# Down projection of an encoder block: where the sums of weight quarters are made

## The chip, the cores and the metric

The kernel runs on one core of a Trainium2 chip. The metric is the device time of one execution in microseconds (us). The kernel before takes 1648.68 us, the median of three runs (1645.87, 1648.68 and 1654.98 us).

## The reference, cut to what matters

Two layers of an encoder on 512 tokens of width 1024, all in float32. A layer is a token mixer (neighbourhood attention in layer 0, dilated attention in layer 1) and a SwiGLU channel mixer with 2816 hidden columns:

```
def swiglu(x, w_gate, w_up, w_down):
    return (jax.nn.silu(x @ w_gate) * (x @ w_up)) @ w_down

x = x + rms_norm(h, norm_mix_post[layer])
h = rms_norm(x, norm_ffn_pre[layer])
x = x + rms_norm(swiglu(h, w_gate, w_up, w_down), norm_ffn_post[layer])
```

The change concerns the last product, hidden (512 x 2816) by `w_down` (2816 x 1024), and what is issued during the two products ahead of it.

## The kernel before, in words

**Exactness.** Every float32 operand is split into a high part and a low remainder (`split`: ScalarE copies and rounds, line 89; VectorE subtracts, line 90). One product is three matmuls: high by high, high by low, low by high (`mm3`, lines 101 to 103).

**Seven products instead of eight.** Each large product is cut into 2 x 2 quarters and done in seven block products from sums of quarters. In the down projection the hidden matrix lies as four quarters `x1a, x1b, x2a, x2b` (two halves of tokens by two halves of the contraction), and `w_down` as four quarters `ga, gb, ua, ub` (two halves of columns by two halves of the contraction). A weight quarter is 128 partitions by 2 x 2816 float32, 2.88 MB. The seven products, in the order of the code, take the weights gb, ga, ga+ua, ga+ua+ub, ub, ua+ub and the sum of all four. Their names in the profile carry p2, p1, d, s2/s4, s3 and x2b.

**Pieces.** `down` (line 582) takes each product in six pieces, five of two 128-row blocks and one of one block. A whole piece is 512 KB of weights and 12 matmuls with 512 columns; a product is 66 matmuls. Products p1, s2, s3 and x2b accumulate in the banks called `left` (tile `yd_s`), p2, d1 and s4 in `right` (`yd_pp`).

**Where the weight sums come from.** Plain quarters are loaded by SyncE (SP) into buffers of 4 KB per partition: four halves of the `raw` tiles (tiles `r_d`), later two more from the arena `raw` (`more`). The sums are made in SBUF: `ga` is loaded whole into the arena `wd` (`mem`, line 648), and GpSimd (POOL) issues accumulating DMAs that add `ua`, then `ub`, then `gb` to it piece by piece (line 600). Each needs the split of the earlier sum to be done. For s3, `ua` is loaded into the ring and `ub` added to it there (lines 606 to 608).

**Gate and up.** `gate_up` (line 538) runs 22 units, each from 1 MB of weights (`load2`, line 85). The raw weights go to two `raw` tiles (`r_gu`) and three places in the arena `fg`. POOL makes two of each unit's weight sums (lines 168 and 169). `fg` is one tile, so what is placed over it after it, the arenas `wd` and `raw`, waits for the last unit's last operation (line 564).

**What sets the order.** Python emits the instructions in program order with the position as priority. A planner (line 1186, `schedule_with_timeline_sim=True`) then puts each engine's instructions in an order by a simulated timeline: of the instructions whose operands and buffers are ready, the earliest in the program goes first. On the chip each engine and each DMA-issuing queue runs that order and stops at any wait. DMAs that POOL issues go through one software queue (queue 0), SP's through a hardware queue (queue 1); both are worked off by the same 16 DMA engines. The kernel's first loads (`x_cols`, `g_mix_pre`, `na_v`; lines 804 to 809) feed the first norm and the value projection (`v_quarter`); the loops over the attention heads use POOL for sums and scalings (lines 168 to 174, 853) and its DMAs for storing and reloading results (`rvd`, lines 757 and 761).

Of the kernel before, what the change touches and what calls it, by code (L numbers as in the profile page):

```python
# [26 lines left out]
QF = FT * P  # L27
# [11 lines left out]
def encoder_kernel(ctx: ExitStack, tc: tile.TileContext, a: dict, out: bass.AP):  # L39
    nc = tc.nc  # L40
# [497 lines left out]
    def gate_up(layer, xs, hid, fg):  # L538
        wg, wu = a["wg"], a["wu"]
        raws = ring(fg, 0, 2 * D, 3)  # L540
        g_, u_, p5_ = ring(fg, 6 * D, 512, 4), ring(fg, 8 * D, 512, 2), ring(fg, 9 * D, 256, 2)
        v_ = w22_ring(rxc[:, 4 * D:5 * D])
        units, us = {}, {}

        def unit_of(f):
            if f in units or f >= FT:
                return units.get(f)
            raw = load2((wg[layer, f], wu[layer, f]), f"gu{layer}_{f}", None if f % 5 < 2 else next(raws))
            b, g = bank(("s", "s", "pp", "o", "pp", "pp")[f % 6], f"gu{layer}_{f}"), next(g_)

            def sink(n, left, other):
                u = us.get(f)
                if n == 0:
                    act.activation(g[:, :256], other, AF.Copy)
                    dve.tensor_add(g[:, :256], g[:, :256], left)
                elif n == 1:
                    act.activation(u[:, :256], other, AF.Copy)
                    dve.tensor_sub(u[:, :256], u[:, :256], left)  # L558
                elif n == 2:
                    dve.tensor_sub(u[:, 256:], other, left)  # L560
                else:
                    act.activation(g[:, :256], g[:, :256], AF.Silu)
                    act.activation(g[:, 256:], left, AF.Silu)
                    dve.tensor_mul(hid[f], *(v.rearrange("p (h c) -> p h c", h=2) for v in (g, u)))

            units[f] = Seven(raw, b, xs, f"{layer}_{f}", sink, None, next(v_), (pool, pool, dve, dve))
            return units[f]

        ahead = 3
        for f in range(ahead):  # L570
            unit_of(f).first()
        for f in range(FT):
            for i in range(f, min(f + 2, FT)):
                if i not in us:
                    us[i], units[i].p5 = next(u_), next(p5_)
            run(unit_of(f), unit_of(f + 1), unit_of(f + ahead))

    def down(layer, hm, hl_, mem, yp, more, sink):
# [7 lines left out]
        ga, gb, ua, ub = (a["wd"][layer, i] for i in range(4))  # L590

        def xp(v, i):
# [5 lines left out]
        def add(v, src):  # L598

            nc.gpsimd.dma_start(v, src, accum_op=ALU.add)  # L600
# [10 lines left out]
        def added(w):  # L611

            for i in range(last + 1):
                add(wp(mem, i), wp(w, i))
                yield wp(mem, i)

        def operands2(x, w, name):
            h, u = next(hl_), wslot(name)
            nx, nw = x.shape[1], w.shape[1]
            return (split(h[:, :nx], h[:, 512:512 + nx], x), split(u[0][:, :nw], u[1][:, :nw], w))  # L620

        def prod(o, ops, start=False, ms=(0, 1)):
            hs_, us = ops
            n = hs_[0].shape[1] // 256
            for m in ms:
                for k in range(n):
                    mm3(o[m], both(hs_, ALL, slice(k * 256 + m * P, k * 256 + m * P + P)),
                        both(us, ALL, slice(k * 512, k * 512 + 512)), start and k == 0, k == n - 1)
# [13 lines left out]
            prod(right, operands2(xp(x1b, i), w, f"{nm}p2_{i}"), i == 0)  # L642
        for m in range(2):
            act.activation(y1g[m], right[m], AF.Copy)

        early = list(loaded(ga[:, :2 * D]))
        for i in (*range(2, last + 1), 0, 1):
            nc.sync.dma_start(wp(mem, i), wp(ga, i))
# [7 lines left out]
        for i in range(last + 1):  # L656
            t = wp(mem, i)
            add(t, wp(ua, i))
            prod(right, operands2(xp(x2a, i), t, f"{nm}d1_{i}"), i == 0)
            dve.tensor_sub(xp(x2a, i), xp(x2a, i), xp(x1a, i))  # L660
        for m in range(2):
            act.activation(p5[m], right[m], AF.Copy)
        ops = None
        for i, w in enumerate(loaded(ub)):
            w0 = wp(ub, i)
            t = wp(mem, i)
            add(t, w0)
            dve.tensor_add(xp(x1b, i), xp(x2a, i), xp(x1b, i))

            dve.scalar_tensor_tensor(xp(x1a, i), xp(x2a, i), -1.0, xp(x2b, i), op0=ALU.mult, op1=ALU.subtract)  # L670
            prod(left, operands2(xp(x2a, i), t, f"{nm}s2_{i}"))
            if ops:
                prod(right, ops)
            ops = operands2(xp(x1b, i), w, f"{nm}s4_{i}")
        for m in range(2):
            act.activation(y1u[m], left[m], AF.Copy)
        prod(right, ops)
# [89 lines left out]
    def ffn(layer, stack):  # L767
        hl_ = ring(rxc, 0, D, 5)
        rxb = None
        with arena(f"hid{layer}", FT * 512, "right") as hm:  # L770
            h2 = hm.rearrange("p (h x) -> p h x", h=2)
            hid = [h2[:, :, f * 256:f * 256 + 256] for f in range(FT)]
            with arena(f"fg{layer}", 9 * D + 512) as fg:
                gate_up(layer, xs, hid, fg)
            with arena(f"ed{layer}", D, "right") as ed, arena(f"yp{layer}", 2 * D, "right") as yp:
                rcomb = ring(ed, 0, 512, 2)

                def sink(t, xt, hs, gn):
# [412 lines left out]
```

## Time and profile before

| | |
|---|---|
| time, median of three | 1648.68 us |
| the profiled execution: its time, its span | 1645.9 us, 1644.1 us |
| mean granted TensorE clock | 0.978 |
| PE busy | 1536.3 us (93% of the span) |
| VectorE, ScalarE, POOL busy | 77%, 52%, 42% |
| moved by DMA | 208.80 MB, 127 GB/s on average |
| gate and up, then down, layer 0 | about 293 to 542, 542 to 657 us of the span |
| gate and up, then down, layer 1 | about 1273 to 1523, 1523 to 1636 us of the span |

The time is what the run took; the span is from the first to the last instruction of the same execution, so 1.8 us lie around it. Rows by stage give busy time per engine with the number of instructions, then the granted clock (PEclk, 1.00 is full), the mean busy share of the 16 DMA engines and what they moved. A chain of waits follows the work that ended last back from the end. A timeline row gives start, duration, engine, source line and operand names; what stands in brackets is the idle time before it and what ended it.

### The profile page before, as it was taken

Reading aid. Unit: us, or ns where it says so; the run is one execution under the profiler, and the core shown is the slowest. Engines: PE = TensorE matmul, PEld = TensorE weight load, DVE = VectorE, ACT = ScalarE, POOL = GpSimd, SP = SyncE. Lnnn points to the kernel's source line nnn. Section 1 sums busy time; section 2 is a strip of 40 time slices with the busy share of each in tenths; the row PEclk is TensorE's granted clock in tenths of the full one; section 3 lists DMA queues with packets and bytes.
Section 4 is the critical chain, followed back from the end, with each engine's and each line's share of the span. In section 5 each row is a group of like instructions: output and inputs, shape, how many; then the busy total and the mean of one; then the engine's idle time right before and its main releaser. Section 6 shows DMA issues by size and latency. Waiting matters only on the chain.

```text
span 1644.1 us, 28158 instructions
## 1 busy us (share of the span) xinstructions
PE 1536.3 (93%) x10788; PEld 1387.7 (84%) x10788; DVE 1263.6 (77%) x2140; ACT 850.2 (52%) x1659; POOL 685.7 (42%) x622
## 2 busy tenths in 40 slices
PE   7999999799999898879999999999998799999896
PEld 7977767799999686879988887888876799999684
DVE  5478864889998877677688788697865699998866
ACT  5356653455555555434465456455553455555554
POOL 3345432733330122465556655565613633330221
PEclk9999999899999999999999999999999899999999
DMA  4322353322322996545321231221545233323994
GB/s 167 118 66 97 122 202 128 141 78 106 120 83 71 251 239 177 175 133 163 116 84 53 78 116 65 104 77 65 195 140 169 88 103 104 103 78 97 251 243 115
DMA packets 66248, 208.80 MB, mean 127 GB/s; under 512 B 7040, under 2 KB 17280, under 8 KB 66112
## 3 DMA queue, kind: packets, MB, share of 16 engines
q1 hardware_dynamic: 53936, 164.91, 29.4%
q0 software_dynamic: 12032, 41.82, 10.6%
q8 instruction: 85, 1.39, 0.4%
q14 instruction: 51, 0.42, 0.1%
q10 hardware_dynamic: 144, 0.26, 0.0%
HBM read 184.94 MB, written 22.02 MB: 126 GB/s over the span
## 4 chain that ended last, share of the span: by engine, by line
PE 65%; DVE 14%; DMA 9%; issue 6%; POOL 3%; ACT 3%; SPq 0%; POOLq 0%; DVEq 0%; ACTq 0%
PE gu L101 9%; PE gu L102 9%; PE gu L103 9%; PE pp_d L101 3%; PE pp_d L103 3%; PE pp_d L102 3%; DMA raw<-wd 3%; DVE ap L911 2%; DMA wd<-wd 2%; PE t L1023 2%; PE yo L101 1%; PE sb L967 1%; PE yo L103 1%; PE yo L102 1%; PE pp_n L101 1%
## 5 line engine op out<-in xcount | busy, mean ns | idle before, releaser
L103 PE MATMUL gu<-rxc,l_a 128*128 128x256 f32 x352 | 102.2, 291 | 2.9 <-DVE l_a L90 2.9
L101 PE MATMUL gu<-rxc,h_a 128*128 128x256 f32 x352 | 102.8, 294 | 0.0
L102 PE MATMUL gu<-rxc,h_a 128*128 128x256 f32 x352 | 102.7, 292 | 0.0
L101 PE MATMUL gu<-rxa,h_c 128*128 128x256 f32 x352 | 100.2, 285 | 0.7 <-DVE fg L558 0.4
L101 PE MATMUL gu<-rxa,h_b 128*128 128x256 f32 x352 | 99.7, 284 | 0.2 <-ACT rxa L324 0.2
L102 PE MATMUL gu<-rxa,h_b 128*128 128x256 f32 x352 | 99.8, 284 | 0.0
L103 PE MATMUL gu<-rxa,l_c 128*128 128x256 f32 x352 | 99.6, 283 | 0.0
L102 PE MATMUL gu<-rxa,h_c 128*128 128x256 f32 x352 | 99.6, 283 | 0.0
L103 PE MATMUL gu<-rxa,l_b 128*128 128x256 f32 x352 | 99.5, 283 | 0.0
L937 ACT ACTIVATE ap<-ap 128x256 f32<-128x256 f32 x128 | 64.0, 502 | 57.0 <-DVE ap L936 56.3
L600 POOL DMA_DIRECT2D wd<-wd x36 | 34.3, 999 | 140.8 <-DVE l_d1p L90 50.3
L168 POOL TENSOR_TENSOR fg<-fg 128x512 f32<-128x512 f32 x24 | 39.8, 1657 | 121.0 <-DVE l_a L90 119.8
L168 POOL TENSOR_TENSOR r_gu<-r_gu 128x512 f32<-128x512 f32 x20 | 35.5, 1773 | 116.3 <-DVE l_a L90 116.3
L168 POOL TENSOR_TENSOR r_d<-r_d 128x512 f32<-128x512 f32 x24 | 38.0, 1584 | 97.7 <-DVE l_ad L90 97.7
L89 ACT ACTIVATE rxc<-hid 128x512 fp32r<-128x512 f32 (+1 forms) x84 | 49.2, 590 | 53.2 <-PE yd_s L102 32.8
L1009 POOL TENSOR_SCALAR ap<-ap 128x256 f32<-128x256 f32 x128 | 69.2, 560 | 15.4 <-DVE ap L927 15.2
L103 PEld LDWEIGHTS gu<-rxc,l_a 128*128 128x128 f32 x352 | 70.2, 199 | 3.1 <-DVE l_a L90 3.1
L101 PEld LDWEIGHTS gu<-rxc,h_a 128*128 128x128 f32 x352 | 70.3, 200 | 0.5 <-ACT rxc L324 0.5
L102 PEld LDWEIGHTS gu<-rxc,h_a 128*128 128x128 f32 x352 | 70.4, 200 | 0.0
L101 PEld LDWEIGHTS gu<-rxa,h_c 128*128 128x128 f32 x352 | 67.5, 192 | 1.7 <-DVE fg L558 1.5
L101 PEld LDWEIGHTS gu<-rxa,h_b 128*128 128x128 f32 x352 | 67.6, 193 | 0.5 <-ACT rxa L324 0.5
L102 PEld LDWEIGHTS gu<-rxa,h_c 128*128 128x128 f32 x352 | 67.5, 192 | 0.2
(590 smaller groups left out, 6366.7 us busy)
## 6 DMA issues: line engine op xcount, KB each, us to landing
r_d<-dil_qk SPq DMA_DIRECT2D x48, 512.0 KB, 4.5
r_d<-wd SPq DMA_DIRECT2D x30, 512.0 KB, 4.5
wd<-wd POOLq DMA_DIRECT2D x30, 512.0 KB, 9.6
fg<-wg SPq DMA_DIRECT2D x24, 512.0 KB, 3.7
fg<-wu SPq DMA_DIRECT2D x24, 512.0 KB, 4.6
r_gu<-wg SPq DMA_DIRECT2D x20, 512.0 KB, 3.7
r_gu<-wu SPq DMA_DIRECT2D x20, 512.0 KB, 4.6
r_n<-na_qk SPq DMA_DIRECT2D x16, 512.0 KB, 4.4
```

Of the source, the lines that this page charges most:

```text
L89: act.activation(h, src, AF.Copy)
L101: i = pe.matmul(o, s[0], m[0], start=start, stop=False, skip_group_check=True)
L102: pe.matmul(o, s[0], m[1], start=False, stop=False, skip_group_check=True)
L103: pe.matmul(o, s[1], m[0], start=False, stop=stop, skip_group_check=True)
L168: e[0].tensor_add(q[0], q[0], q[2])
L600: nc.gpsimd.dma_start(v, src, accum_op=ALU.add)
L911: dve.tensor_copy(out_[32 * k:32 * k + 32, :, i], in_[32 * i:32 * i + 32, :, k])
L937: act.activation(pr[:, f], pr[:, f], AF.Exp, bias=st[:, c + i:c + i + 1], scale=-1.0, accum_out=st[:, 8 + c + i:9 + c + i])
L967: pe.matmul(s[:, f0:f0 + P], qf[rw, block(c)], kf[rw, block(c)], start=True, stop=True)
L1009: pool.tensor_scalar(v, v, w[:, 4 * hd + b:4 * hd + b + 1], 1.0, op0=ALU.mult, op1=ALU.mult)
L1023: pe.transpose(t[:, block(i)], part(a_b, *blocks[4 * n + i]), ident)
```

## The change

Per layer four tiles in DRAM (`wsum`, 128 x 5632 float32 each) receive ga+ua, ga+ua+ub, ua+ub and the sum of all four. `wd_sums` gives six steps that `gate_up` emits ahead of units 0, 3, 6, 9, 12 and 15. A step is a plain DRAM-to-DRAM copy or an accumulating DMA into DRAM, two halves of 1.44 MB for each operand, all issued by POOL. `down` no longer has `mem` and no accumulating DMAs: it loads each of its seven operands by SP, into a ring of ten places, the four halves of the `raw` tiles and six from the arena `raw`, which is now the only one over `fg`.

```diff
         ahead = 3
+        sums = wd_sums(layer)
         for f in range(ahead):
             unit_of(f).first()
         for f in range(FT):
+            if f % 3 == 0 and f // 3 < len(sums):
+                sums[f // 3]()
...
+    wsum = [dpool.tile([4, P, 2 * QF], F32, name=f"wsum{i}") for i in range(2)]
+
+    def wd_sums(layer):
+        ga, gb, ua, ub = (a["wd"][layer, i] for i in range(4))
+        gu, gub, uab, every = (wsum[layer][i] for i in range(4))
+
+        def step(*pairs, op=None):
+            for o, v in pairs:
+                for h in range(2):
+                    c = slice(h * QF, h * QF + QF)
+                    if op is None:
+                        nc.gpsimd.dma_start(o[:, c], v[:, c])
+                    else:
+                        nc.gpsimd.dma_start(o[:, c], v[:, c], accum_op=op, max_dma_last_dim=2 * QF)
+
+        return [partial(step, (gu, ga), (uab, ua)), partial(step, (gu, ua), (uab, ub), op=ALU.add),
+                partial(step, (gub, gu)), partial(step, (gub, ub), op=ALU.add),
+                partial(step, (every, gub)), partial(step, (every, gb), op=ALU.add)]
...
-        raw_ = cycle(raws)
+        raw_ = cycle(raws + [more[:, i * D:i * D + D] for i in range(6)])
...
-        def loaded(w, more=None):
-            for i in range(w.shape[1] // D + (w.shape[1] % D > 0)):
-                c = slice(i * D, min((i + 1) * D, w.shape[1]))
-                v = next(raw_)[:, :c.stop - c.start]
-                nc.sync.dma_start(v, w[:, c])
-                if more is not None:
-                    add(v, more[:, c])
+        def loaded(w):
+            for i in range(last + 1):
+                v = next(raw_)[:, :wp(w, i).shape[1]]
+                nc.sync.dma_start(v, wp(w, i))
                 yield v
...
-        early = list(loaded(ga[:, :2 * D]))
-        for i in (*range(2, last + 1), 0, 1):
-            nc.sync.dma_start(wp(mem, i), wp(ga, i))
-        for i in range(last + 1):
-            w = early[i] if i < len(early) else wp(mem, i)
+        for i, w in enumerate(loaded(ga)):
             prod(left, operands2(xp(x1a, i), w, f"{nm}p1_{i}"), i == 0)
...
-        raw_ = cycle(raws + [more[:, i * D:i * D + D] for i in range(2)])
-        for i in range(last + 1):
-            t = wp(mem, i)
-            add(t, wp(ua, i))
-            prod(right, operands2(xp(x2a, i), t, f"{nm}d1_{i}"), i == 0)
+        for i, w in enumerate(loaded(gu)):
+            prod(right, operands2(xp(x2a, i), w, f"{nm}d1_{i}"), i == 0)
...
-        for i, w in enumerate(loaded(ub)):
-            w0 = wp(ub, i)
-            t = wp(mem, i)
-            add(t, w0)
+        for i, (w, w0) in enumerate(zip(loaded(gub), loaded(ub))):
...
-            for i, w in enumerate(loaded(ua, ub) if n == 0 else added(gb)):
+            for i, w in enumerate(loaded(uab if n == 0 else every)):
...
-                with arena(f"wd{layer}", 2 * QF) as mem, arena(f"raw{layer}", 2 * D) as more:
-                    end = down(layer, hm, hl_, mem, yp, more, sink)
+                with arena(f"raw{layer}", 6 * D) as more:
+                    end = down(layer, hm, hl_, yp, more, sink)
```

More of the change, by code (lines that the diff above doesn't have):

```diff
@@ L576, in gate_up, with down @@
             run(unit_of(f), unit_of(f + 1), unit_of(f + ahead))
-    def down(layer, hm, hl_, mem, yp, more, sink):
+    wsum = [dpool.tile([4, P, 2 * QF], F32, name=f"wsum{i}") for i in range(2)]
[13 more added lines that the diff above has]
+                partial(step, (every, gub)), partial(step, (every, gb), op=ALU.add)]
+    def down(layer, hm, hl_, yp, more, sink):
         left, right = ([bank(u, f"yd{layer}_{u}{m}") for m in range(2)] for u in ("s", "pp"))
@@ L588, in down @@
         raws = [r[:, i * D:i * D + D] for i in range(2) for r in raws]
-        raw_ = cycle(raws)
+        raw_ = cycle(raws + [more[:, i * D:i * D + D] for i in range(6)])
         ga, gb, ua, ub = (a["wd"][layer, i] for i in range(4))
+        gu, gub, uab, every = (wsum[layer][i] for i in range(4))
         def xp(v, i):
@@ L596, in wp @@
             return v[:, pieces[i].start * 512:pieces[i].stop * 512]
-        def add(v, src):
-            nc.gpsimd.dma_start(v, src, accum_op=ALU.add)
-        def loaded(w, more=None):
-            for i in range(w.shape[1] // D + (w.shape[1] % D > 0)):
-                c = slice(i * D, min((i + 1) * D, w.shape[1]))
-                v = next(raw_)[:, :c.stop - c.start]
-                nc.sync.dma_start(v, w[:, c])
-                if more is not None:
-                    add(v, more[:, c])
+        def loaded(w):
+            for i in range(last + 1):
+                v = next(raw_)[:, :wp(w, i).shape[1]]
+                nc.sync.dma_start(v, wp(w, i))
                 yield v
-        def added(w):
-            for i in range(last + 1):
-                add(wp(mem, i), wp(w, i))
-                yield wp(mem, i)
         def operands2(x, w, name):
@@ L654, in down @@
             dve.tensor_add(y1g[m], y1g[m], left[m])
-        raw_ = cycle(raws + [more[:, i * D:i * D + D] for i in range(2)])
-        for i in range(last + 1):
-            t = wp(mem, i)
-            add(t, wp(ua, i))
-            prod(right, operands2(xp(x2a, i), t, f"{nm}d1_{i}"), i == 0)
+        for i, w in enumerate(loaded(gu)):
+            prod(right, operands2(xp(x2a, i), w, f"{nm}d1_{i}"), i == 0)
             dve.tensor_sub(xp(x2a, i), xp(x2a, i), xp(x1a, i))
@@ L663, in down @@
         ops = None
-        for i, w in enumerate(loaded(ub)):
-            w0 = wp(ub, i)
-            t = wp(mem, i)
-            add(t, w0)
+        for i, (w, w0) in enumerate(zip(loaded(gub), loaded(ub))):
             dve.tensor_add(xp(x1b, i), xp(x2a, i), xp(x1b, i))
             dve.scalar_tensor_tensor(xp(x1a, i), xp(x2a, i), -1.0, xp(x2b, i), op0=ALU.mult, op1=ALU.subtract)
-            prod(left, operands2(xp(x2a, i), t, f"{nm}s2_{i}"))
+            prod(left, operands2(xp(x2a, i), w, f"{nm}s2_{i}"))
             if ops:
                 prod(right, ops)
-            ops = operands2(xp(x1b, i), w, f"{nm}s4_{i}")
+            ops = operands2(xp(x1b, i), w0, f"{nm}s4_{i}")
         for m in range(2):
```

## The prediction

> **What bounds the kernel now.** First the page: engines, and the chain that ended last.
>
> ```profile
> PE 1536.3 (93%) x10788; PEld 1387.7 (84%) x10788; DVE 1263.6 (77%) x2140; ACT 850.2 (52%) x1659; POOL 685.7 (42%) x622
> PE 65%; DVE 14%; DMA 9%; issue 6%; POOL 3%; ACT 3%; SPq 0%; POOLq 0%; DVEq 0%; ACTq 0%
> ```
>
> PE bounds the whole, but 9% of the chain is DMA. Next the stages of the two down projections (PE busy, PEld, DVE, ACT, POOL, clock, DMA share, GB/s), cut where PE's products change:
>
> ```profile
> 562.90:568.50 5.60, 0.03 (x2) 0.01 (x1) 4.37 (x9) 1.52 (x2) 0.00 (x0) 0.89 1.07 212
> 568.50:586.60 18.10, 18.06 (x67) 14.28 (x68) 15.82 (x21) 10.24 (x14) 6.03 (x7) 0.85 1.06 202
> 586.60:616.40 29.80, 29.80 (x133) 24.66 (x132) 20.05 (x24) 18.69 (x30) 8.41 (x10) 1.00 0.99 252
> 616.40:637.40 21.00, 17.95 (x67) 12.58 (x65) 10.88 (x16) 8.36 (x14) 2.95 (x4) 0.92 0.97 264
> 637.40:656.80 19.40, 16.30 (x78) 13.69 (x79) 18.07 (x26) 15.27 (x28) 6.29 (x3) 1.00 0.22 78
> 1544.20:1549.80 5.60, 0.01 (x1) 0.00 (x0) 4.55 (x8) 1.51 (x2) 0.00 (x0) 0.74 1.06 209
> 1549.80:1567.10 17.30, 17.24 (x67) 13.72 (x68) 15.73 (x21) 10.22 (x14) 5.97 (x7) 0.89 1.06 199
> 1597.00:1635.80 38.80, 32.48 (x132) 23.80 (x131) 23.73 (x33) 17.48 (x31) 5.04 (x4) 1.00 0.52 131
> ```
>
> The third row is what an undisturbed product costs: 133 matmuls in 29.80 us, 0.224 us each, so 66 take 14.8 us. Around it PE loses time in two places per layer while the DMA engines are full at only about 205 GB/s: it stands for 5.6 us and then runs d1 on a lowered clock, and it crawls through s3. The chain of waits in layer 0 says what is late:
>
> ```profile
> 545.51 6.06 DMA wd<-wd
> 555.33 12.03 DMA wd<-wd
> 612.17 9.49 DMA raw<-wd
> 622.19 11.39 DMA raw<-wd
> ```
>
> These are a load, then an accumulating DMA of ga+ua (before d1), and a load and an accumulating DMA of ua+ub (in s3).
>
> **What down gains.** Without accumulating DMAs down loads 42 pieces, 7 x 2.88 = 20.2 MB, in 7 x 14.8 = 104 us, 194 GB/s. What plain loads and accumulating DMAs reach when they fill the engines:
>
> ```profile
> 550.00:555.00 5.00, 5.00 (x24) 4.14 (x23) 3.05 (x3) 4.41 (x6) 1.66 (x2) 1.00 1.02 410
> 565.00:570.00 5.00, 1.47 (x3) 0.75 (x4) 3.77 (x6) 1.21 (x2) 0.01 (x1) 0.72 1.06 211
> ```
>
> At 410 GB/s loads are no bound. The two losses go: 5.6 + (18.1 - 14.8) + (21.0 - 15.0) = 14.9 us in layer 0. In layer 1, 5.6 + 2.5 and 38.8 - 29.6 = 9.2, from which I take 3.1 that isn't the DMA's (the idle PE time of the row 637.40 in layer 0, where DMA is at 0.22): 14.2 us. **Together -29.1 us.** Lower end: if a ring of ten places runs dry, half of it.
>
> **What down loses at its start.** Before, p2's last pieces and p1's first two use the four halves of `raw` again as they come free. Now, places 5 to 10 lie over `fg`, so only four pieces of p2 can be there before gate and up ends.
>
> ```profile
> 520.00:542.20 22.20, 10.11 (x42) 7.72 (x43) 0.00 (x0) 0.00 (x0) 1.00 0.51 147
> 542.20:552.80 10.60, 6.09 (x25) 4.42 (x24) 0.00 (x0) 0.00 (x0) 1.00 0.89 319
> 542.19 1.06 ACT L89 ACTIVATE h_d0p<-r_d 128x1024 fp32r<-128x1024 f32 x1 [1.52 <-PE gu L102]
> 544.42 0.68 DVE L564 TENSOR_TENSOR hid<-fg 128x512 f32<-128x512 f32 x1
> 545.14 2.99 SPq L648 DMA_DIRECT2D wd<-wd  x6
> fg<-wg SPq DMA_DIRECT2D x24, 512.0 KB, 3.7
> raw<-wd SPq DMA_DIRECT2D x4, 512.0 KB, 10.4
> ```
>
> (The first two rows count tile `yd_pp` alone.) By 542.2 PE has done 42 of the 48 matmuls of four pieces; six are left, 1.4 us, and it runs dry at 543.6. `fg` ends at 545.1; the split at 542.19 ahead of it, of a piece of ga that won't be there yet, drops out, so I put the load at 544.1. It lands 3.7 us later, the row of a load on free engines, and is split in 1.06: PE goes on at about 549.0. That is 5.4 us idle, and after such an idle d1 lost another 3.3 and 2.5 us, on average 2.9: 8.3 us a layer, **+16.6 us**. Ends: 5.4 without the slow start, 15.0 with the crowded landing of 10.4 us.
>
> In layer 0 the ring also holds both `raw` tiles until x2b's last pieces are split, where the next layer's values used to be loaded earlier:
>
> ```profile
> 622.48 6.16 SPq L85 DMA_DIRECT2D r_d<-dil_v  x4
> 648.62 0.62 ACT L89 ACTIVATE h_d0x2b<-wd 128x512 fp32r<-128x512 f32 x1
> 649.86 1.06 ACT L89 ACTIVATE h_d<-r_d 128x1024 fp32r<-128x1024 f32 x1 [0.62 <-ACT h_d0x2b L89]
> 656.80:668.00 11.20, 7.97 (x63) 7.15 (x61) 9.74 (x14) 4.73 (x11) 2.97 (x4) 1.00 0.81 277
> ```
>
> The load comes after about 651 and is split near 657 instead of 649.86. Of these 7 us PE's idle 3.2 after 656.8 take half: **+3.5 us** (0 to 7). Down and its end together: -29.1 + 16.6 + 3.5 = **-9.0 us**.
>
> **What the sums cost depends on when they are issued.** By the program, during gate and up. But the planner takes what is ready, and step 0 of both layers is ready at time 0: it reads inputs, writes DRAM and needs no buffer. That ready work goes far ahead of its place the trace shows:
>
> ```profile
> 3.08 0.44 SPq L809 DMA_DIRECT2D ea<-x_cols  x1
> 3.56 0.94 SPq L85 DMA_DIRECT2D r_n<-na_v  x2
> 9.47 0.33 SPq L809 DMA_DIRECT2D ea<-x_cols  x1
> 1203.68 0.33 SPq L85 DMA_DIRECT2D r_gu<-wg  x1
> 1245.62 0.34 SPq L1102 DMA_DIRECT2D ep<-spill  x1
> 5.76 0.56 POOL L308 TENSOR_TENSOR rs_a<-v_a,mhalf 128x1 f32<-128x1 f32 x1 [4.47 <-DVE v_a L304]
> ```
>
> A later value quarter is loaded before the last x_cols, and gate and up's first weights 42 us before the spill that precedes them in the program; only buffers held them. POOL is idle for 4.47 us until 5.76. I therefore expect the eight copies of step 0, 4 x 2.88 = 11.5 MB, in the kernel's first microseconds, and the rest as soon as each predecessor lands.
>
> *At the start* they meet these stages:
>
> ```profile
> 0.00:12.00 12.00, 2.56 (x10) 2.08 (x10) 4.27 (x7) 6.04 (x8) 1.80 (x8) 1.00 0.85 305
> 12.00:42.00 30.00, 28.96 (x236) 28.46 (x237) 17.86 (x23) 15.74 (x27) 13.07 (x10) 1.00 0.30 106
> ```
>
> The engines are full until 12 us, and PE is dense from there. Up to the last x_cols nine loads of 0.52 MB are needed, 4.7 MB; with the copies 16.2 MB, 40 us at 410 GB/s. Do loads and copies take turns? The crowded load above took 10.4 us against 3.7, a factor 2.8; taking turns one row of 4 KB each beside accumulating rows, which need twice a load's time (410 against 211), would be 3. A copy row is 11 KB, so loads get 4/15 and the last x_cols lands near 42 us instead of 14. With 4 us of norm and transposes, by 46 us PE can have done three of four token blocks of two value quarters: 6 x 24 matmuls x 0.123 us (28.96/236) = 18 us, where it has now done 33. **+16 us**, rounded up from 15. Ends: 5 if each queue gets half the bytes, 28 (11.5 MB at 410) if the copies go through first. The Trainium skill, "DMA: Bandwidth & Descriptors", section "Queues, rings and completion order", says that an engine drains a whole packet of some 9 to 17 descriptors before it turns to another queue. By that rule a copy's eight rows per engine would pass between two load rows, and this term would lie at 28; the factor 2.8 speaks for one by one.
>
> *After that* the chain has 23 MB of copies (56 us at 410) and 23 MB of accumulation (112 us at 205), and POOL, which works in order, must wait for each predecessor between its own sums. Rows of POOL's waits, in down now and in the attention stage:
>
> ```profile
> POOL r_d L600 <- DMA r_d<-wd: 18.9, 3, 8.7
> POOL wd L600 <- DMA wd<-wd: 10.7, 1, 10.7
> POOL raw L600 <- DMA raw<-wd: 8.7, 2, 6.4
> POOL r_n L168 <- DVE l_an L90: 27.0, 7, 7.2
> ```
>
> Six waits took 38.3 us, 6.4 each. POOL comes 3.9 us early to a unit's sums; what is behind the wait are these sums, and PE behind them. Five hand-overs from step to step at 6.4 - 3.9 = 2.5 give **+12 us**. Ends: 0, if the planner prices the transfers so that nothing waits; 56 us, if it prices accumulation at the speed of copies (112 - 56). The issues themselves (0.55 to 0.9 us each) vanish in POOL's idle 58%; without it they would be some 25 us.
>
> **Sum:** -9.0 + 16 + 12 = +19 us on the profiled execution's 1645.9 us (span 1644.1), about 1665. That execution lies 2.8 us under the median, so the median should be near **1667 us**.
>
> **The rivals.**
> *Paced as written (faster).* The steps stay at units 0 to 15. Gate and up has room:
>
> ```profile
> 300.00:515.00 215.00, 209.96 (x1723) 208.48 (x1723) 194.79 (x238) 115.03 (x197) 83.49 (x46) 0.99 0.25 87
> ```
>
> A layer's share is 28 + 56 = 84 us of full engines in 215, so 0.25 becomes 0.64, and POOL is idle 131 us. At most 2 us lost: 1645.9 - 9.0 + 1 + 2.8 = 1641 down to 1636 with a smaller stall at down's start; 1638. It decides if the planner holds back work of later program parts, for which no row speaks. 0.25.
> *Moved ahead, but harmless.* The first loads win their turns (+5) and POOL's waits fit its gaps (+3): 1648.68 - 9 + 8 = 1648. 0.17.
> *POOL's queue decides.* The planner's transfers are much too fast, and the sums of the attention units stand behind DMA waits: 12 becomes 45, 1700. The stores and reloads of `rvd` on the same queue would join in. 0.14.
> *Down still waits for data* (the change doesn't do what it says): half of 29.1 stays, 1682. Speaks against it: 194 of 410 GB/s. 0.02.
>
> **How the numbers follow.** The forecast has 0.42, with its own range of 1655 to 1690 from the start's 5 to 28. About 0.5% (8 us) is what a measurement of this kernel can tell from no change. Faster by more: the paced case and a little of the harmless one, 0.27. Within: 0.18. Slower: forecast, POOL's queue and dry ring, 0.55. The range of 1634 to 1702 takes in the paced case and the middle of POOL's.
>
> **What would show it.** The place of the `wsum` copies on POOL: in the first 10 us, or after 290. The first value matmul (now 11.24 us) near 25, and the last x_cols landing near 40. POOL waits for DMAs at the attention stage. In down: no `wd` tile, no idle of 5.6 us before d1, s3 dense, but an idle stretch of 5 us in p2 after gate and up. If the copies stand at their units, the forecast is wrong by its two largest terms.

## The result, and the profile after

The changed kernel takes **1713.38 us**, the median of four runs (1713.08 to 1716.29), against 1648.72 us of the kernel before in the same comparison: 1.0391 times as long, 95% interval 1.0359 to 1.0423. The prediction was 1667 us, within 1634 to 1702: the sign was right, and the time lies outside the range.

First the page of the kernel after: the engines, the DMA engines' busy tenths and GB/s in 40 slices of 42.8 us, and the issues (count, KB each, median us to landing).

```profile
PE 1557.3 (91%) x10788; PEld 1405.2 (82%) x10788; DVE 1266.6 (74%) x2140; ACT 852.4 (50%) x1659; POOL 674.4 (39%) x606
...
DMA  9999933541322156454532132221262522331662
GB/s 357 248 288 261 268 102 119 188 185 62 121 102 100 50 197 205 159 190 131 174 125 80 50 109 77 87 99 63 77 233 78 179 100 99 100 108 66 215 223 98
...
wsum<-wd POOLq DMA_DIRECT2D x24, 1408.0 KB, 27.1
wsum<-wsum POOLq DMA_DIRECT2D x8, 1408.0 KB, 29.7
```

The 32 transfers that make the sums were to run during gate and up. The row of DMA tenths shows them in the first five slices: the engines are full from the start to about 210 us, and no later slice stands out for it. Where the time went is seen by stages. The start of the first and the end of the last matmul of a stage's tile (`vp_n` the values and `pp_n` the attention of layer 0, `gu` gate and up, `yd_s` down), read from the two traces, in us to about the nearest whole one:

| | value stage | attention | gate and up, 0 | down ends, 0 | gate and up, 1 | down ends, 1 |
|---|---|---|---|---|---|---|
| before | 11 to 66 | 66 to 227 | 293 to 542 | 657 | 1273 to 1523 | 1636 |
| after | 19 to 98 | 99 to 312 | 381 to 627 | 733 | 1350 to 1597 | 1702 |

By the end of the value stage the kernel is 32 us late, at the end of attention 85, at gate and up 88. Each down projection then gives 8 to 9 back. The value and attention stages as rows, first of before, then of after (PE, PEld, DVE, ACT, POOL busy and their instructions, clock, DMA share, GB/s):

```profile
0.00:66.00 66.00, 55.52 (x445) 54.54 (x446) 30.27 (x37) 30.40 (x45) 20.04 (x22) 1.00 0.41 145
66.00:227.00 161.00, 154.41 (x1000) 126.44 (x1000) 125.20 (x282) 99.07 (x227) 78.08 (x98) 0.98 0.33 109
```

```profile
0.00:98.00 98.00, 65.13 (x448) 61.88 (x448) 28.35 (x33) 26.99 (x41) 30.05 (x37) 0.90 1.01 296
98.00:312.00 214.00, 168.85 (x987) 135.82 (x988) 133.06 (x283) 101.57 (x224) 93.71 (x113) 0.85 0.73 204
```

The same matmuls take 33 us of idle PE in the value stage in place of 10, and 45 in place of 7 in attention; beside that they are busy 24 us longer, on a granted clock of 0.90 and 0.85. The loads of these stages and the copies share the DMA engines one row for one row. The queues of after from 15 to 45 us (packets, MB, share of the engines), with the landing of the values' loads:

```profile
q0 software_dynamic: 838, 8.38, 73.2%
q1 hardware_dynamic: 842, 3.06, 27.1%
...
r_n<-na_v SPq DMA_DIRECT2D x4, 512.0 KB, 24.7
```

838 packets of POOL's queue beside 842 of SP's; without those of 4 bytes that end a transfer these are 744 rows of 11 KB and 746 of 4 KB. Equal counts alone could also come from several rows of each in turn. The single packets of the trace tell: a packet starts within 5 ns of another's end where an engine goes from one to the next. Where just one packet fits, 580 of 582 copy rows are followed by one of SP's queue, and all 579 load rows by one of POOL's. The loads get 3.06 MB in 30 us, 102 GB/s, and one lands after 24.7 us (the median of four), where the trace of before has 6.2 for the same loads. POOL meanwhile stands behind its own transfers. Its waits and PE's longest in the first 400 us (total, times, longest), and then the timeline around that longest stall (start, duration, operation, and in brackets the idle time and what ended it):

```profile
POOL wsum L594 <- DMA wsum<-wd: 53.7, 6, 17.2
...
PE pp_n L101 <- ACT h_an L89: 27.2, 2, 25.5
...
POOL wsum L596 <- DMA wsum<-wsum: 23.1, 2, 20.4
```

```profile
113.04 0.63 ACT L89 ACTIVATE ao<-r_n 128x512 fp32r<-128x512 f32 x1 [13.11 <-DMA r_n<-na_qk]
...
119.40 1.20 POOL L596 DMA_DIRECT2D wsum<-wd  x1 [20.39 <-DMA wsum<-wsum]
123.35 1.15 POOL L596 DMA_DIRECT2D wsum<-wd  x1 [2.74 <-DMA wsum<-wsum]
124.10 1.69 POOL L168 TENSOR_TENSOR r_n<-r_n 128x512 f32<-128x512 f32 x1
...
128.49 1.06 ACT L89 ACTIVATE h_bn<-r_n 128x1024 fp32r<-128x1024 f32 x1 [14.83 <-POOL r_n L170]
129.46 1.04 ACT L89 ACTIVATE h_an<-r_n 128x1024 fp32r<-128x1024 f32 x1
```

Both suspects stand in these few lines. A weight lands late (113.04), and the sums of weight quarters behind it (line 168) wait on POOL for a copy of step 2, until 124.10; PE goes on at 130.5. Which of the two costs the time the rows can't say: had POOL not waited, the load would still have been late, and the other way round.

In down, the change does what it was to do. The rows of layer 0 from gate and up's end to down's end, and PE's only wait of note there:

```profile
629.30:633.70 4.40, 0.00 (x0) 0.00 (x0) 1.12 (x3) 1.58 (x3) 0.00 (x0) 0.92 0.89 296
633.70:641.20 7.50, 7.45 (x19) 5.44 (x20) 5.33 (x6) 4.57 (x6) 0.00 (x0) 0.59 1.01 392
641.20:732.00 90.80, 90.28 (x402) 74.58 (x401) 78.20 (x106) 58.25 (x92) 9.28 (x6) 1.00 0.58 186
```

```profile
PE yd_pp L101 <- ACT h_d0p L89: 4.4, 1, 4.4
```

The stops ahead of d1 and inside s3 are gone (90.28 busy in 90.80); the new stop at p2 is there, 4.4 us and a slow product behind it.

### The profile page after: what moved, and what is told of

Read it like the earlier page. It is cut to its first block, busy times and chain, and to the rows that moved or that the text cites. A ratio compares the mean times of both kernels' runs of the same rounds, so it can differ in the third digit from the quotient of the medians.

```text
span 1711.3 us, 28129 instructions
## 1 busy us (share of the span) xinstructions
PE 1557.3 (91%) x10788; PEld 1405.2 (82%) x10788; DVE 1266.6 (74%) x2140; ACT 852.4 (50%) x1659; POOL 674.4 (39%) x606
## 4 chain that ended last, share of the span: by engine, by line
PE 59%; DVE 10%; issue 3%; DMA 2%; ACT 2%; POOL 2%; SPq 0%; POOLq 0%; DVEq 0%; ACTq 0%
PE gu L101 8%; PE gu L102 8%; PE gu L103 8%; PE pp_d L101 4%; PE pp_d L103 3%; PE pp_d L102 3%; DVE ap L912 2%; PE yd_s L101 2%; PE yd_s L102 2%; PE yd_s L103 2%; PE yd_pp L101 2%; PE yd_pp L102 2%; PE t L1024 2%; PE yd_pp L103 2%; PE sb L968 2%
## 5 line engine op out<-in xcount | busy, mean ns | idle before, releaser
L103 PE MATMUL gu<-rxc,l_a 128*128 128x256 f32 x352 | 102.5, 291 | 1.9 <-DVE l_a L90 1.9
L89 ACT ACTIVATE rxc<-hid 128x512 fp32r<-128x512 f32 (+1 forms) x84 | 49.2, 593 | 62.8 <-PE yd_s L102 31.5
L1010 POOL TENSOR_SCALAR ap<-ap 128x256 f32<-128x256 f32 x128 | 69.2, 560 | 18.5 <-DVE ap L928 18.3
L101 PEld LDWEIGHTS gu<-rxa,h_b 128*128 128x128 f32 x352 | 67.6, 193 | 1.6 <-ACT rxa L324 1.6
```

The source lines that it names most:

```text
L89: act.activation(h, src, AF.Copy)
L101: i = pe.matmul(o, s[0], m[0], start=start, stop=False, skip_group_check=True)
L103: pe.matmul(o, s[1], m[0], start=False, stop=stop, skip_group_check=True)
L1010: pool.tensor_scalar(v, v, w[:, 4 * hd + b:4 * hd + b + 1], 1.0, op0=ALU.mult, op1=ALU.mult)
```

## The experiments

All ratios are to the kernel before, run beside it. In several kernels no sums are made, so that down multiplies by other weights; where that is so, the run's own text or the sentence before it says it.

### Down and the sums apart

Three kernels: down's new loads without any sums, the sums kept at their written places, and the eight copies of step 0 alone. The first and the third make no sums.

```diff
# e2_down_alone
-        sums = wd_sums(layer)
...
-            if f % 3 == 0 and f // 3 < len(sums):
-                sums[f // 3]()
...
-        gu, gub, uab, every = (wsum[layer][i] for i in range(4))
+        gu, gub, uab, every = ua, ub, ua, gb
# e1_pinned
-                        nc.gpsimd.dma_start(o[:, c], v[:, c])
+                        i = nc.gpsimd.dma_start(o[:, c], v[:, c])
...
+                    tc.keep_in_program_order(i)
# e3_copies_first
-        return [partial(step, (gu, ga), (uab, ua)), partial(step, (gu, ua), (uab, ub), op=ALU.add),
...
+        return [partial(step, (gu, ga), (uab, ua))]
```

> No sums are made: down loads the plain quarters ua, ub, ua and gb in their place, as many bytes in the same order; the additions of weight quarters are left out. It shows what the new down is worth by itself. Theory P: 1649 - 18 = about 1631 us, 4 to 5 us of idle PE after gate and up in each layer. Rival D (part of the 18 us is only stages shifted against each other, as in the forecast's 9): 1638 to 1642 us.

> The changed kernel, but each of the 32 DMAs of the sums is pinned behind the POOL instruction that precedes it in the program, so it stays at its unit of gate and up. Theory P (the early place of the sums costs 85 us in the first 380 us, down itself gains 18): 1713 - 85 = about 1630 us, the first attention stage as long as before (gate and up begins near 293 us), gate and up at most 3 us longer. Rival G (the sums' 46 MB cost PE time wherever they run, by crowding the loads and by POOL's waits ahead of the units' sums): gate and up 15 to 40 us longer per layer, 1660 to 1710 us.

> Of the sums only the eight copies of step 0 (11.5 MB, ready at time 0) are left, nothing waits for them; down loads plain quarters for the two later sums; the additions are left out. Against e2_down_alone it prices the copies beside the first loads. Theory W (POOL standing at waits for DMAs is most of the 85 us): 15 to 22 us over e2, about 1650. Rival C (full DMA engines are most of it): the whole 31 us by which the value stage ended later, 1660 or more.

Down alone: 1631.02 us, 0.9909 (0.9893 to 0.9926). Sums at their places: **1633.39 us, 0.9919 (0.9889 to 0.9949)**, 2.4 over down alone, which is within the scatter of its own runs (1625.89 to 1640.40), so the sums cost little there and the change is a gain. Step 0's copies at the start: 1641.45, 0.9961 (0.9942 to 0.9979), 10.4 over down alone; the value stage runs from 19 to 84 us, 18 later than before, and 8 of these come back later. That is less than either theory gave.

With the sums at their places the engines are as full as at the start of after, and PE doesn't mind. A stretch of gate and up in e1_pinned, with its queues and landings:

```profile
320.00:400.00 80.00, 77.33 (x624) 76.65 (x624) 64.41 (x80) 38.82 (x67) 32.71 (x25) 0.97 1.02 288
```

```profile
q0 software_dynamic: 2338, 16.49, 79.7%
q1 hardware_dynamic: 1770, 6.46, 21.5%
...
fg<-wg SPq DMA_DIRECT2D x4, 512.0 KB, 9.8
```

The loads get 6.46 MB in 80 us, 81 GB/s, and land after 9.8 us, and PE works 77.33 of 80: gate and up needs no more, and it has five places for raw weights ahead of it. So neither full engines nor a slow landing is a loss by itself; it depends on the stage they meet. The loss of the whole, 82 us over down alone, comes from the sums' place in time, and 72 of it from the 24 transfers of steps 1 to 5, which e3 doesn't have.

### The transfers without the waits

e4 has 32 plain copies with nothing between them to wait for (no sums are made). e5 moves the same bytes in eight transfers, e8 half as many again.

```diff
# e4_copies_no_wait
+        o = [wsum[layer][i] for i in range(8)]
+        return [partial(step, (o[0], ga), (o[2], ua)), partial(step, (o[4], ua), (o[5], ub)),
...
# e5_copies_eight
+            nc.gpsimd.dma_start(o[:, :, c].rearrange("q p c -> p q c"), v[:, :, c].rearrange("q p c -> p q c"))
...
+        w = [wsum[layer][4 * i:4 * i + 4] for i in range(2)]
+        v = a["wd"][layer, :4]
# e8_traffic_of_after
+        w = [wsum[layer][6 * i:6 * i + 6] for i in range(2)]
+        v = a["wd"].rearrange("l q p c -> (l q) p c")[2 * layer:2 * layer + 6]
```

> All sixteen operand transfers per two layers are plain copies into DRAM tiles of their own, 46 MB, all ready at time 0 and none waiting for another; the additions are left out and down loads four of the copies. The engines are full for some 150 us, but POOL never stands at a wait for them. Theory W: little over e3, 1650 to 1662 us. Rival C: engines that are full cost by themselves, 1690 or more.

e4: 1756.84 us, 1.0673 (1.0651 to 1.0694). It wasn't what it was meant to be: POOL did wait. POOL's timeline in e4, then its waits and VectorE's in the first 180 us:

```profile
3.38 2.56 POOL L594 DMA_DIRECT2D wsum<-wd  x5
11.99 0.52 POOL L594 DMA_DIRECT2D wsum<-wd  x1 [6.05 <-DMA wsum<-wd]
17.28 0.52 POOL L594 DMA_DIRECT2D wsum<-wd  x1 [4.78 <-DMA wsum<-wd]
...
49.07 0.58 POOL L308 TENSOR_TENSOR rs_a<-v_a,mhalf 128x1 f32<-128x1 f32 x1
```

```profile
POOL wsum L594 <- DMA wsum<-wd: 102.5, 24, 6.1
...
DVE ea L315 <- POOL rs_a L308: 84.8, 4, 55.7
```

Eight issues, and then each of the other 24 waits until an earlier one has landed. The norm's last step (`rs_a`, line 308) stands behind them until 49.07 us; in the kernel before it ran at 5.76. So the run mixed the two suspects, and eight transfers are the way to part them.

> The same 46 MB of plain copies, DRAM to DRAM, ready at time 0, in the same rows of 11 KB, but in 8 transfers of 5.77 MB in place of 32 of 1.44 MB; the sums aren't made, so down computes with other data. With eight transfers GpSimd issues all of them in the first microseconds and then has none left to wait behind. Theory W (the time went to GpSimd's in-order waits between its transfers): the traffic alone is left; it lasts some 46.1 MB at 275 GB/s = 168 us, the value stage is as late as with the eight copies alone (+18), and the first attention stage, whose transfers moved 109 GB/s on average before, gets about the 100 GB/s that it needs: 1645 to 1665. Theory C (the time went to the DMA engines being full, whoever waits for what): as long as the run of 32 transfers, 1757, or at the least over 1690. Between 1665 and 1690 the two share it.

> Eight plain copies as in the run of eight transfers, half as large again (8.45 MB each, 67.6 MB in all), for which GpSimd never waits. That is the DMA time of the changed kernel's sums: 16 copies of 1.44 MB, and 16 accumulating transfers of 1.44 MB whose rows of 5.6 KB took as long as a copy's rows of 11 KB (440 against 422 to 431 ns), so 23 MB and twice 23 MB. The sums aren't made. Theory T (the transfers alone are the loss): by the two runs so far, 11.5 MB cost 10.4 us and 46.1 MB 58.3 us over down alone, 1.38 us for each MB; 67.6 MB then cost 88, so 1705 to 1730, the changed kernel's own 1713 or more. Theory W (GpSimd's waits add a good part): 1640 to 1695, as the loads get by with their share once the first 45 us are over.

e5: 1689.35 us, 1.0246 (1.0209 to 1.0282). e8: 1727.34 us, 1.0493 (1.0418 to 1.0568). Against e4 the waits were worth 67 us; but the same bytes with no wait of POOL's cost 58 over down alone, in the gap that e5's text called shared, and a traffic that takes the DMA engines about as long as the changed kernel's sums costs 96. (Its eight transfers are 8.65 MB each by the trace's 8448 KB, 69.2 MB in all; its text has 8.45 and 67.6.) e8 overstates it, since POOL's own stores go through the same queue and stood behind these transfers ("ACT ao L749 <- DMA rvd<-ao", 32.3 us once). Theory W, that only the waits matter, is out. How late loads cost, e5 shows in its first 110 us:

```profile
POOL rs_a L308 <- DVE v_a L304: 39.5, 2, 24.7
...
ACT vmem L89 <- DMA r_n<-na_qk: 21.2, 1, 21.2
...
DVE v_a L304 <- ACT ea L313: 19.0, 4, 7.7
...
ACT h_n L89 <- DMA r_n<-na_v: 14.0, 2, 10.3
```

The last of the first loads, the fourth x_cols, landed at 45.7 us (15.7 before), which is most of the delay. Its squares ran on ScalarE only at 54.99, as ScalarE stood 7.3 us for a product of PE ahead of them. VectorE waits for the squares, and POOL's norm for VectorE: the fourth `rs_a` ran at 56.40 us (23.16 before). So a late load delays its own work, and in an engine that works in order a wait also delays work whose data had landed.

### The waits without the stage's work behind them

The other way round: the changed kernel, but the work of layer 0 that stood behind POOL's waits on other engines.

```diff
# e7_qk_sums_on_vector
-        return Seven(raw, b, xs, name, sink, p5, v, (pool, pool, pool, pool), 0)
+        return Seven(raw, b, xs, name, sink, p5, v, (dve, dve, dve, dve), 0)
# e10_off_pool_after (layer 0 alone; e9_off_pool_alone has the same without sums)
+        return Seven(raw, b, xs, name, sink, p5, v, ((dve if name[0] == "n" else pool),) * 4, 0)
...
+                nc.scalar.dma_start(rvd[layer][j].bitcast(F32), mem.bitcast(F32))
...
-        pool.tensor_copy(q[:, :, 0:64], q[:, :, SEQ:].bitcast(F32))
+        act.activation(q[:, :, 0:64], q[:, :, SEQ:].bitcast(F32), AF.Copy)
...
+                act.activation(views[i], views[i], AF.Copy, scale=rc[:, i:i + 1])
```

> The changed kernel whole, with one thing moved: the four sums of weight quarters of each query-key unit (14 units sum on GpSimd between 66 and 227 us before, 41 us of work there) are made on VectorE, so no weights of the attention stage stand behind a waiting transfer on GpSimd. VectorE was busy 125 of those 161 us and gets some 20 us more. Theory W: of the +52 that the first attention stage showed, most goes, 35 to 45, and VectorE gives a few back: 1665 to 1690. Theory C: nothing that GpSimd held up mattered, the loads are late all the same: 1705 to 1725.

e7: 1722.31 us, 1.0446 (1.0406 to 1.0485), no gain, and the figure of Theory C. Its rows beside those of after show why it says less than hoped. First after, then e7, and e7's wait:

```profile
100.00:130.00 30.00, 4.31 (x22) 4.11 (x22) 2.38 (x4) 2.13 (x3) 7.62 (x7) 0.57 1.03 304
130.00:200.00 70.00, 59.13 (x348) 48.17 (x348) 45.02 (x90) 32.35 (x73) 36.05 (x41) 0.84 1.03 271
```

```profile
100.00:130.00 30.00, 20.14 (x126) 19.22 (x127) 13.98 (x22) 6.62 (x11) 2.78 (x3) 0.77 1.02 317
130.00:200.00 70.00, 45.68 (x260) 35.91 (x259) 37.53 (x91) 28.29 (x65) 18.63 (x29) 0.78 1.03 262
```

```profile
PE s L447 <- POOL rxc L841: 24.0, 2, 23.8
```

The stall of 25 us was gone and 16 us of PE's work came back. In the next stretch 13 were lost to the next thing behind POOL's waits, the copy of the queries (line 841). Gate and up starts at 375 in place of 381 us, and layer 1, whose sums moved too, loses more than that. So all of it had to move.

> The base for the next run: down alone (no sums, 1631), with most of GpSimd's work in the first attention stage moved: its sums of weight quarters to VectorE, the scaling of the softmax and the copy of the queries to ScalarE, the stores of the heads' outputs to ScalarE's queue. 1630 to 1655; the moves may cost some, as VectorE was busy 125 and ScalarE 99 of 161 us there.

> The changed kernel whole, sums and all, with the same work moved off GpSimd in the first attention stage, so that nothing of that stage stands behind a waiting transfer. To be compared with down alone under the same moves: the changed kernel stood 82 over down alone. Theory T (the transfers themselves are the loss, through the late loads): 65 to 85 over its base. Theory W (the waits on GpSimd are the loss): 15 to 35 over its base.

e9: 1633.75 us, 0.9895 (0.9864 to 0.9927): the moves cost next to nothing. e10: 1699.70 us, 1.0325 (1.0252 to 1.0399), 66 over its base, where the changed kernel is 82 over down alone. This is Theory T's figure (65 to 85), at its lower end.

### Shorter rows

If an engine takes one row from each queue in turn, a copy's row of 11 KB (422 ns in the trace) beside a load's of 4 KB (159 ns) is what starves the loads, and shorter rows give their share back.

```diff
# e11_short_rows_46 (e5 with other rows)
+            nc.gpsimd.dma_start(*(t.rearrange("q p c -> (q p) c")[:, c] for t in (o, v)), max_dma_last_dim=QF)
# e12_after_short_rows
-                        nc.gpsimd.dma_start(o[:, c], v[:, c])
+                        nc.gpsimd.dma_start(o[:, c], v[:, c], max_dma_last_dim=QF)
...
-                        nc.gpsimd.dma_start(o[:, c], v[:, c], accum_op=op, max_dma_last_dim=2 * QF)
+                        nc.gpsimd.dma_start(o[:, c], v[:, c], accum_op=op, max_dma_last_dim=QF)
```

> The 46.1 MB of plain copies in eight transfers again (1689 us, 58 over down alone), in rows of 2.8 KB in place of 11 KB; no sums. Theory R (each DMA engine takes one row from each queue in turn, so the long rows are what starves the loads): a load's row of 4 KB took 159 ns and a copy's of 11 KB 422 to 431, a loads' share of 27% where both wait; a row of 2.8 KB should take a quarter of that, some 107 ns, and leave loads 60%. The loads then get over 200 GB/s, about what the value stage took before, and 40 of the 58 us come back: 1640 to 1660. Rival B (the queues share by bytes, or the copies as a whole fill the engines whatever their rows): 1680 to 1695.

> The changed kernel whole, its copies and accumulating transfers in rows of 2.8 KB (11 KB and 5.6 KB before). Theory R: a copy's row then takes some 107 ns and an accumulating row some 220 ns beside a load's 159, so loads get 42 to 60% of the engines' time in place of 27%, and half or more of the 66 us that the transfers cost goes; GpSimd's waits stay: 1660 to 1690. Rival B: 1705 to 1725.

The rows came out as 5.6 KB for plain copies (215 ns each) and 2.8 KB for accumulating ones (234 ns), so half the length, not a quarter. e11: 1677.30 us, 1.0153 (1.0019 to 1.0287), 12 less than e5. e12: 1711.80 us, 1.0361 (1.0222 to 1.0501), the same as after. By their times Theory R failed: e12 is at Rival B's figure, e11 lies between the two. By the rows the turns are as it said. The queues of e12 from 15 to 45 us, beside those of after above:

```profile
q0 software_dynamic: 1506, 7.98, 67.0%
q1 hardware_dynamic: 1123, 4.08, 34.5%
...
r_n<-na_v SPq DMA_DIRECT2D x4, 512.0 KB, 12.0
```

Found as above, all 693 load rows are followed by one of POOL's, while 289 of 1038 POOL rows are followed by another of POOL's: there no load was waiting, so the counts are no longer equal. The loads get 4.08 MB in place of 3.06 and land after 12.0 us in place of 24.7. The time didn't follow, because POOL then was the later one: e12's fourth `rs_a` ran at 59.70 us, behind POOL's waits, as in after (59.04). In e11 it was POOL again, in a new way (its waits in the first 60 us):

```profile
POOL wsum L591 <- issue: 18.0, 2, 17.6
```

Its eighth issue took 17.6 us in which it waited for nothing that the profile shows, and the norms stood behind it until 31.53. So short rows alone were covered by POOL's waits; what they are worth shows only with these waits out of the way.

### Both taken away

```diff
# e13_off_all_alone, e14_off_all_long_rows, e15_off_all_short_rows: as e9 and e10, and for layer 0's first norms
+        if name[0] == "a":
+            act.activation(r, v, AF.Sqrt)
+            dve.reciprocal(r, r)
...
+            (dve if name[0] == "a" else pool).tensor_sub(d1, ha, hb)
```

> The base of the next two: down alone, without sums, with the attention stage's work off GpSimd as before (1634), and the value stage's too: the norm's reciprocal root as a root on ScalarE and a reciprocal on VectorE, and the four combinations of token blocks on VectorE. 1632 to 1645.

> The changed kernel with both stages' work off GpSimd, so that up to gate and up nothing but the sums' own transfers waits there; rows of 11 and 5.6 KB as they are. What is left is the loads that share the DMA engines with the sums. Theory M (each cause alone is enough): 50 to 75 over its base, 1685 to 1715. Theory W (the waits are the cause, the loads only look slow): at most 25 over its base.

> The same with the sums' rows cut to 2.8 KB, which brought the first loads' landing from 14.8 to 10.1 us and the value quarters' from 27.5 to 12.5 in the runs before. Theory M: with both causes gone most of the loss is gone, 10 to 35 over its base, 1645 to 1675. Theory T (full DMA engines cost the same whatever the rows and waits): 1685 to 1715.

| | us | ratio | over e13 | values | attention | gate and up starts |
|---|---|---|---|---|---|---|
| e13, no sums | 1626.14 | 0.9877 (0.9830 to 0.9924) | | 11 to 66 | 66 to 217 | 287 |
| e14, long rows | 1694.19 | 1.0290 (1.0252 to 1.0329) | 68 | 19 to 85 | 87 to 290 | 361 |
| e15, short rows | 1677.10 | 1.0187 (1.0148 to 1.0226) | 51 | 14 to 75 | 77 to 274 | 344 |

With nothing behind POOL's waits but the transfers themselves and, late in the stage, the reloads of `rvd`, the transfers still cost 68 of the 82 us. The landing of a weight of the attention stage in the first 100 us, in e13 and then in e14, and PE's largest wait in e14's attention stage:

```profile
r_n<-na_qk SPq DMA_DIRECT2D x10, 512.0 KB, 4.4
```

```profile
r_n<-na_qk SPq DMA_DIRECT2D x4, 512.0 KB, 22.6
...
PE pp_n L101 <- ACT h_an L89: 17.7, 5, 8.3
```

The split that PE waits for (`h_an`) itself stood 12.8 us for loads ("ACT h_an L89 <- DMA r_n<-na_qk"). **The loads that share the DMA engines are the larger cause**, enough for most of the loss alone; POOL's waits on top of them add some 14. Shorter rows, now uncovered, give 17 back, most of it in the value stage. Both theories of e15 missed: Theory M wanted at most 35 left, 51 are, and 1677 is faster than Theory T's range. The attention stage of e13, then of e15:

```profile
66.00:218.00 152.00, 145.01 (x962) 121.20 (x960) 120.49 (x284) 111.98 (x263) 2.81 (x5) 0.98 0.30 103
```

```profile
77.00:274.00 197.00, 172.04 (x988) 138.93 (x987) 134.87 (x317) 121.42 (x282) 16.58 (x18) 0.88 0.91 243
```

It is 45 us longer: 27 of them are busy time, on a clock of 0.88 in place of 0.98 and with 26 more matmuls recorded, and 18 idle time. The longest wait, 7.2 us, is for a reload of `rvd`, which POOL issues. How much of the lower clock follows from the broken work was not tried.

### A version that beats both

> The kernel with the sums kept at their written places (1633.4 us, 0.992 of before), and beside it the order of down's staging buffers: the first eight pieces go into the four halves that the gate-up ring gives back first, twice over, and only then into the six of the new buffer, which the layer's mixer data hold until gate-up ends. Theory D (down's start is late because its fifth piece and those behind it wait for the new buffer's memory): the idle of 6.2 us ahead of the second run of down's first product goes, and the slow first product (7.5 us for 18 matmuls) becomes dense (4.2): 7 to 9 a layer, so 1615 to 1622, 0.980 to 0.985 of before. Rival: the start is late because of the weights themselves (the DMA engines, or SyncE's queue): 1630 to 1637.

```diff
# e6_pinned_early: e1_pinned, and
-        raw_ = cycle(raws + [more[:, i * D:i * D + D] for i in range(6)])
+        raw_ = chain(raws, raws, cycle([more[:, i * D:i * D + D] for i in range(6)] + raws))
```

**1620.34 us, 0.9823 (0.9798 to 0.9847)**, 13 less than e1. Down's start and its first products in layer 0:

```profile
530.00:550.00 20.00, 19.98 (x113) 17.21 (x112) 13.51 (x18) 10.18 (x16) 0.00 (x0) 1.00 0.52 148
550.00:612.00 62.00, 61.49 (x272) 50.29 (x272) 52.87 (x73) 39.48 (x60) 0.63 (x1) 1.00 0.77 260
```

No stop is left: the pieces that waited for the new buffer's memory now use again the halves that come free during gate and up. Theory D stands.

## Why the prediction was wrong, by its own steps

**The issue at time 0: right.** The prediction said that the planner would issue step 0 of both layers in the first microseconds, and the rest as soon as each predecessor lands. The copies went out from 1.27 and 3.36 us on, and the last of the 32 transfers at 194 us.

**The start, +16: right in mechanism, near in size.** Taking turns row by row was its estimate, with 4 of 15 parts for the loads: 109 of 410 GB/s; 102 were measured. The last x_cols was to land near 42 us; it was issued at 14.48 and landed 31.0 us later, at 45.5. The eight copies alone put the value stage 18 us back, but cost 10 over the whole. The factor 2.8, on which the prediction chose between one row and several, can't choose: a load of 128 rows has eight for each of the 16 engines as well, and eight of each in turn give the same shares and the same 16. The order of the single packets above decides, and it is one for one. The Trainium skill, "DMA: Bandwidth & Descriptors", section "Queues, rings and completion order", says that an engine drains a packet of some 9 to 17 descriptors from one queue before it goes to the next. The trace doesn't agree: 580 of 582 and 579 of 579 rows are followed by the other queue. The prediction's 28 by that rule let the copies pass eight rows and the loads only one.

**"After that", +12: the step that failed.** The prediction had written down that 23 MB of copies (56 us at 410) and 23 MB of accumulation (112 us at 205) would follow: 168 us of full engines. It then priced them by POOL's hand-overs alone, as if the loads of these 168 us went on undisturbed; the turns that it had just used for the first 42 us it dropped for the rest. By its own share, 109 GB/s, the attention stage gets what it needs on average (109 in the row of before), which may be why it looks harmless; but the stage loads in bursts (between 0 and 295 GB/s in slices of 4 us before) into two tiles, and in after one of its weights landed after 24.0 us in the first 100 (4.5 before). In numbers: transfers without POOL's waits cost 68 (e14 over e13), of which the first term covers 16; the missing 52 are this step (58, if the first term is taken as the 10 of e3). The Trainium skill, "DMA: Bandwidth & Descriptors", section "Issuing engines are not separate DMA queues", says that transfers from the scalar, sync and gpsimd engines run on the same 16 engines and interleave. The runs agree: beside the transfers a weight of attention landed after 22.6 us in e14, 4.4 in e13.

**POOL's hand-overs: near in size, by luck.** +12 was forecast, some 14 were measured (82 less 68). The forecast had five hand-overs of 2.5 us each; the trace has waits of up to 20.4 us, 77 us in all (53.7 and 23.1), so the 14 isn't five times 2.5. The rival in which POOL's queue decides gave 1700, the nearest figure of all, by a mechanism that holds a sixth of the loss: with the work taken off POOL, 66 to 68 us stay. Where POOL's waits stand ahead of the norms, though, as in e4, they cost 67 more (e4 less e5).

**Down, -9.0: right in its parts, too small in the gain.** From gate and up's end to down's end, layer 0 took 114.4 us before and 104.9 after, layer 1 112.2 and 104.0: together -17.7. The stall at p2 was put at 5.4 of idle and 2.9 of slow start; it is 4.4, and then 19 matmuls in 7.45 us where they take 4.3 (0.224 each), 3.2 more: 15.2 for two such layers against 16.6. The later load of the next layer's values (+3.5) isn't seen: from down's end to `vd` it is 35.5 us before and 36.2 after. That leaves some 33 for the gain that was put at 29.1. Down alone as a kernel gives 16 (1646.98 less 1631.02), where the forecast had 9.

**The paced rival: the alternative that was offered.** It gave 1638 for sums at their places; e1_pinned took 1633.39. The condition named for it, that the planner holds work of later parts back, didn't hold until it was forced.

## What to carry to other kernels

Price a background transfer for as long as it lasts, in every stage that it meets: a mean need in GB/s didn't tell the stage that lost (109, two tiles to load into) from the one that didn't (87, five places). That the number of places loaded ahead makes the difference is a reading of these two stages; no run varied it. Work with no operands to wait for is issued at once by a planner that takes what is ready; pin it to its place. Where two causes cover each other, an experiment that takes one of them away shows too little (14 of 82 us for POOL's waits, 2 for short rows); take both away (31 for the two together, e15), and then put back one.

## What the runs showed of the hardware that was not expected

In this program POOL had at most eight transfers under way; the ninth issue waited until an earlier one had landed (24 waits, 102.5 us in all, e4). Whether the chip or the program's semaphores set the eight was not tried. With twice the rows in a transfer (e11), an issue of POOL's, the eighth, stood for 17.6 us with no wait that the profile names. It went out at 30.00 us, 0.7 after the last packet of the first of the seven before it (29.28); in e5, with half the rows, all eight were out by 7.7 us. That a bound on rows under way holds it is a guess. An accumulating row into DRAM took about twice as long for its bytes as a plain one: 440 ns for 5.6 KB against 422 ns for 11 KB, and at half the lengths 234 ns for 2.8 KB against 215 ns for 5.6 KB.
